# Both feed-forward products of a hybrid transformer layer, as seven half-size products each

## The chip, the cores and the metric

The kernel runs on one core of a Trainium2 chip, in one launch. Its metric is the device time in microseconds of that core; lower is better. Times of the kernel before: 2298.93 us in the median of three runs, from 2298.3 to 2300.44.

A core has a matrix engine (TensorE; PE in the profile, and PEld where it loads weights), three engines for elementwise work (VectorE or DVE, ScalarE or ACT, GpSimd or POOL), and SyncE (SP), which here only issues DMAs. Each works through its own queue in order and waits on semaphores. TensorE writes to PSUM, eight banks of 128 x 512 float32; everything else lies in SBUF or in DRAM.

## The reference

One layer on 1024 tokens of width 1024: a norm, three token mixers (a gated convolution, a stick-breaking attention, a cross-attention into 256 memory tokens) with sigmoid gates, an output projection, and the feed-forward block that this case is about. All in float32:

```python
merged = gates[:, :, 0] * y_conv + gates[:, :, 1] * y_sb + gates[:, :, 2] * y_x
x = x + merged @ w_out[l]

h2 = rms_norm(x, g_mlp[l])
x = x + jnp.square(jax.nn.relu(h2 @ w_up[l])) @ w_down[l]
```

`w_up` is 1024 x 4096 and `w_down` 4096 x 1024. The two products of the feed-forward block are 2 x 1024 x 1024 x 4096 multiply-adds.

## The kernel before

**Precision.** TensorE takes its operands in a rounded float32 type (`F32R`). To keep float32's accuracy every operand is split into a high part (a cast on ScalarE, lines 89 and 113) and a low part (the original less the high part, on VectorE, lines 90 and 114), and every product of tiles is three products: high x high, high x low, low x high (`mm3`, line 121, and `mm3_steps`, line 201, which does the same in steps between which other work is issued). A product is 128 x 128 by 128 x 512. I call the products that go into one PSUM bank one after the other a chain.

**Memory.** `pgp` holds 40 pages of 128 x 1024 float32 (`page`), `rawp` four raw weight tiles of that size (`load`, line 81, on the SP queue), `whlp` three pairs of split weights, `hpp` three half-width tiles. The PSUM banks are handed out as three `d`, two `z`, two `t` and one `o`.

**Order.** The program is written in one order, and a scheduler turns it into one queue per engine: it follows the written order where work is ready by its own estimate, and lets ready work pass work that waits. An instruction given to `keep_in_program_order` (line 93) stays behind those given to it earlier on its engine. Before, only the weight splits of the first stage were (`pin`).

**Stages.** Lines 316 to 723 make the projections, the attentions, the gates and the convolution. Lines 726 to 753 multiply the branches with the gates into `mT`. Lines 770 to 797 add `merged @ w_out` to `x`: `acc[t]`, eight tiles of 128 tokens, in two halves `ch` of the columns. In the second half every finished row block is normalized (`normed`, line 153: square and sum on ScalarE, a power on GpSimd, a scaling on VectorE), and the first four blocks are transposed on TensorE into `h2`, between the chains of the last three blocks (`norm_transpose`, line 172). `h2[k][th]` is block `k` of 128 model columns by half `th` of the tokens, high and low.

**Feed-forward, lines 800 to 835.** Eight chunks of 512 hidden columns. In a chunk, the up part makes four column blocks by two token halves, each a chain of 24 products (eight blocks `k`, three products), reads PSUM with a relu on ScalarE, squares and splits. The second half of the tokens is transposed between the products of the second chain of all. The down part runs over two halves of the output columns and eight token blocks, each a chain of 12 products, which VectorE adds to `acc[t]` (line 833); in the last chunk the sum goes out at once. Hidden values stay in SBUF.

Of the kernel before, what the change touches and what calls it, by code (L numbers as in the profile page):

```python
# [16 lines left out]
P = 128  # L17
# [5 lines left out]
NXH = 4  # L23
NM = M // P
FF = 4096
NCHUNK = FF // 512
EPS = 1e-6


# [7 lines left out]
def f32v(ap):  # L37

    return ap.bitcast(F32)
# [3 lines left out]
def block_kernel(ctx, tc, x, mem, small, w_in, w_v, w_kv, w_co, w_so, w_xo, w_out, w_up, w_dn, out):  # L43
# [19 lines left out]
    def page(dt=F32R, shape=(P, 1024)):  # L63
        return pgp.tile(list(shape), dt, tag="pg", name=nm("pg"))
# [41 lines left out]
    def unit(src, paged=False):  # L106

        return halves(load(src), paged)
# [63 lines left out]
    def norm_transpose(rows, dst, gcol):  # L172

        n = len(rows) * P
        for k in range(KT):
            tp = pt()
            for i, r in enumerate(rows):
                nc.tensor.transpose(tp[:, i * P : (i + 1) * P], r[:, k * P : (k + 1) * P], ident)
# [576 lines left out]

    acc = [None] * 8
    rows = []
    h2 = [None] * KT

    def h2_dst(th):  # L760
        def dst(k):
            if th == 0:
                h2[k] = {}
            t_ = page(F32R, (P, 2, 512))
            h2[k][th] = (t_[:, 0, :], t_[:, 1, :])
            return h2[k][th]

        return dst

    for ch in range(2):  # L770
        s = slice(ch * 512, ch * 512 + 512)
        while len(wo) < 4 * ch + 4:
            wo.append(unit(w_out[ch, len(wo) - 4 * ch], True))
        for t in range(8):
            th, i = t // 4, t % 4
            if ch == 0:
                acc[t] = page(F32)
                nc.sync.dma_start(out=acc[t], in_=x[t * P : (t + 1) * P, :])
            ps = pd()
            steps = mm3_steps(  # L780
                ps,
                [
                    (cut(mT[k, th], i * P, (i + 1) * P), cut(wo[4 * ch + k // 2], (k % 2) * 512, (k % 2) * 512 + 512))
                    for k in range(KT)
                ],
                4,
            )
            if ch == 1 and t == 5:
                more = norm_transpose(rows[0:4], h2_dst(0), C_GMLP)
            if ch == 1 and t >= 5:  # L790
                for _ in steps:
                    fill(more, 1)
            run(steps)
            nc.vector.tensor_tensor(out=acc[t][:, s], in0=ps, in1=acc[t][:, s], op=ALU.add)
            if ch == 1:
                rows.append(normed(acc[t]))
    run(more)


    for c in range(NCHUNK):  # L800
        f = {}
        for j2 in range(2):
            ws = [unit(w_up[4 * c + 2 * j2 + j]) for j in range(2)]
            for th, j in ((0, 0), (0, 1), (1, 0), (1, 1)):
                w = ws[j]
                ps = pd()
                steps = mm3_steps(ps, [(cut(w, k * P, (k + 1) * P), h2[k][th]) for k in range(KT)], KT)
                if (c, j2, th, j) == (0, 0, 0, 1):
                    weave(steps, norm_transpose(rows[4:8], h2_dst(1), C_GMLP))
                run(steps)  # L810
                r = hpp.tile([P, 512], F32, tag="hp", name=nm("r"))
                nc.scalar.activation(r, ps, AF.Relu)
                t_ = page(F32R, (P, 2, 512))
                f[2 * j2 + j, th] = (t_[:, 0, :], t_[:, 1, :])
                nc.scalar.activation(t_[:, 0, :], r, AF.Square)
                nc.vector.tensor_tensor(out=r, in0=r, in1=r, op=ALU.mult)
                nc.vector.tensor_tensor(out=t_[:, 1, :], in0=r, in1=f32v(t_[:, 0, :]), op=ALU.subtract)
        for ch in range(2):
            us = [unit(w_dn[c, ch, kp]) for kp in range(2)]
            s = slice(ch * 512, ch * 512 + 512)  # L820
            for t in range(8):
                ps = pd()
                mm3(
                    ps,
                    [
                        (
                            cut(f[j, t // 4], (t % 4) * P, (t % 4 + 1) * P),
                            cut(us[j // 2], (j % 2) * 512, (j % 2) * 512 + 512),
                        )
                        for j in range(4)  # L830
                    ],
                )
                nc.vector.tensor_tensor(out=acc[t][:, s], in0=ps, in1=acc[t][:, s], op=ALU.add)  # L833
                if c == NCHUNK - 1:
                    nc.sync.dma_start(out=out[t * P : (t + 1) * P, s], in_=acc[t][:, s])


def _layout(i):
# [10 lines left out]
    def per_part(v):  # L849
# [9 lines left out]
    w_dn = a["w_down"][0].reshape(NCHUNK, 2, 2, P, 2, 512).transpose(0, 4, 1, 3, 2, 5)  # L859
    return {  # L860
        "x": a["x"][0],
        "mem": a["mem"][0],
# [9 lines left out]
        "w_dn": w_dn.reshape(NCHUNK, 2, 2, P, 1024),  # L872
    }


# [17 lines left out]
```

## Time and profile before

| what | value |
|---|---|
| median of three runs | 2298.93 us |
| the profiled execution's time | 2298.66 us |
| its span, first to last instruction | 2297.0 us |
| TensorE busy | 2261.7 us (98%) |
| VectorE busy | 1127.5 us (49%) |
| ScalarE busy | 801.7 us (35%) |
| GpSimd busy | 298.2 us (13%) |
| granted TensorE clock, mean | 1.000 |
| DMA traffic | 174.79 MB, mean 76 GB/s |

The profile is one execution. A row of a group names the line, the engine, the operation, what it writes and reads, the shapes and the count; then the time that the engine was busy with it, the mean of one in ns, and the idle time ahead of it with what ended it. A row of the timeline gives start and duration in us, and in brackets the idle time ahead. TensorE's products overlap: the distance of two starts is what one costs, not its duration.

### The profile page before, as it was taken

What the parts mean: (1) busy time and instruction counts of PE and PEld (TensorE: products, weight loads), DVE (VectorE), ACT (ScalarE), POOL (GpSimd) and SP (SyncE); (2) the same over time, 40 slices, a digit from 0 to 9 for tenths busy, and PEclk for the clock granted to TensorE, in tenths of its full rate; (3) what the DMA queues carried; (4) which work ended last, traced back from release to release, by engine and by line L of the source; (5) the groups of instructions that cost most, each with busy time, mean ns of one, the idle gap of its engine ahead of it and who ended that gap; (6) DMA issues with size and microseconds to landing.
All of it is one profiled execution on the core that took longest, in us unless ns stands there. A gap on an engine that the chain in (4) does not pass through costs nothing.

```text
span 2297.0 us, 26957 instructions
## 1 busy us (share of the span) xinstructions
PE 2261.7 (98%) x10688; PEld 1882.5 (82%) x10688; DVE 1127.5 (49%) x1589; ACT 801.7 (35%) x1550; POOL 298.2 (13%) x422
## 2 busy tenths in 40 slices
PE   7999999999999999999999999999999999999999
PEld 7988888778788788888888888888888888888887
DVE  5533128787778778753333344434433333333333
ACT  6544226565555656532111121213221211221220
POOL 1021113333333333310000000000000000000000
PEclk9999999999999999999999999999999999999999
DMA  6311322222221222211112443250111111111111
GB/s 220 101 56 69 127 64 71 83 77 71 74 92 56 92 74 67 81 46 46 56 46 74 147 156 118 94 183 1 43 50 56 37 55 56 37 56 54 39 46 74
DMA packets 49455, 174.79 MB, mean 76 GB/s; under 512 B 6065, under 2 KB 6065, under 8 KB 49329
## 3 DMA queue, kind: packets, MB, share of 16 engines
q1 hardware_dynamic: 42160, 147.90, 20.5%
q0 software_dynamic: 7168, 25.17, 2.9%
q8 instruction: 84, 1.38, 0.2%
q14 instruction: 43, 0.34, 0.0%
HBM read 135.29 MB, written 29.36 MB: 72 GB/s over the span
## 4 chain that ended last, share of the span: by engine, by line
PE 85%; DVE 5%; issue 3%; ACT 3%; POOL 3%; DMA 1%; SPq 0%; POOLq 0%; ACTq 0%; DVEq 0%
PE d L207 17%; PE d L206 17%; PE d L205 17%; PE d L125 9%; PE d L126 9%; PE d L127 9%; POOL pg L558 2%; PE o L597 2%; DVE pg L114 1%; PE t L582 1%; DVE pg L572 1%; PE z L554 1%; PE z L553 1%; DVE whl L90 1%; ACT pg L555 1%
## 5 line engine op out<-in xcount | busy, mean ns | idle before, releaser
L205 PE MATMUL d<-pg,whl 128*128 128x512 f32 x1664 | 656.0, 394 | 0.0
L207 PE MATMUL d<-pg,whl 128*128 128x512 f32 x1664 | 649.1, 390 | 0.0
L206 PE MATMUL d<-pg,whl 128*128 128x512 f32 x1664 | 649.0, 390 | 0.0
L207 PEld LDWEIGHTS d<-pg,whl 128*128 128x128 f32 x1664 | 312.3, 188 | 66.5
L205 PEld LDWEIGHTS d<-pg,whl 128*128 128x128 f32 x1664 | 312.6, 188 | 60.6
L206 PEld LDWEIGHTS d<-pg,whl 128*128 128x128 f32 x1664 | 312.7, 188 | 60.4
L89 ACT CAST whl<-raw 128x1024 fp32r<-128x1024 f32 x160 | 168.6, 1054 | 518.4 <-PE d L127 306.6
L90 DVE TENSOR_TENSOR whl<-raw,whl 128x1024 fp32r<-128x1024 f32 x160 | 200.0, 1250 | 293.4 <-ACT whl L89 292.6
L558 POOL TENSOR_SCALAR_AFFINE_SELECT pg<-pg 128x128 f32<-128x128 f32 x256 | 167.9, 662 | 304.8 <-ACT pg L555 293.9
L568 DVE TENSOR_TENSOR_SCAN pg<-pg,zero 128x128 f32<-128x128 f32 (+7 forms) x128 | 177.4, 1386 | 57.4 <-POOL pg L558 54.7
L125 PE MATMUL d<-whl,pg 128*128 128x512 f32 x512 | 199.2, 389 | 0.0
L126 PE MATMUL d<-whl,pg 128*128 128x512 f32 x512 | 199.2, 389 | 0.0
L127 PE MATMUL d<-whl,pg 128*128 128x512 f32 x512 | 199.2, 389 | 0.0
L113 ACT CAST pg<-t 128x256 fp32r<-128x256 f32 (+2 forms) x336 | 115.2, 368 | 203.7 <-DVE pg L114 141.4
L833 DVE TENSOR_TENSOR pg<-d,pg 128x512 f32<-128x512 f32 x128 | 88.3, 690 | 188.7 <-PE d L127 188.5
L114 DVE TENSOR_TENSOR pg<-t,pg 128x256 fp32r<-128x256 f32 (+2 forms) x336 | 129.3, 404 | 65.5 <-ACT pg L113 62.0
L125 PE MATMUL d<-pg,whl 128*128 128x512 f32 x384 | 149.4, 389 | 0.0
L126 PE MATMUL d<-pg,whl 128*128 128x512 f32 x384 | 149.4, 389 | 0.0
L127 PE MATMUL d<-pg,whl 128*128 128x512 f32 x384 | 149.4, 389 | 0.0
L205 PE MATMUL d<-pg,pg 128*128 128x512 f32 (+1 forms) x384 | 138.5, 361 | 0.6 <-ACT pg L116 0.5
L206 PE MATMUL d<-pg,pg 128*128 128x512 f32 (+1 forms) x384 | 137.5, 359 | 0.5 <-DVE pg L90 0.5
L207 PE MATMUL d<-pg,pg 128*128 128x512 f32 (+1 forms) x384 | 137.5, 359 | 0.0
(114 smaller groups left out, 2755.4 us busy)
## 6 DMA issues: line engine op xcount, KB each, us to landing
raw<-in_w_in SPq DMA_DIRECT2D x72, 512.0 KB, 3.7
raw<-in_w_up SPq DMA_DIRECT2D x32, 512.0 KB, 3.6
raw<-in_w_dn SPq DMA_DIRECT2D x32, 512.0 KB, 4.1
gscr<-pg POOLq DMA_DIRECT2D x24, 512.0 KB, 3.0
raw<-gscr SPq DMA_DIRECT2D x24, 512.0 KB, 3.5
raw<-in_w_kv SPq DMA_DIRECT2D x16, 512.0 KB, 4.4
pg<-in_x SPq DMA_DIRECT2D x16, 512.0 KB, 8.7
pg<-pg SPq DMA_DIRECT2D x32, 256.0 KB, 4.0
```

The source lines that it names most:

```text
L89: a = nc.scalar.copy(hl[0], raw)
L90: b = nc.vector.tensor_tensor(out=hl[1], in0=raw, in1=f32v(hl[0]), op=ALU.subtract)
L113: nc.scalar.copy(hi, src)
L114: nc.vector.tensor_tensor(out=lo, in0=src, in1=f32v(hi), op=ALU.subtract)
L125: nc.tensor.matmul(ps, lhsT=ah, rhs=bh, start=i == 0, stop=False)
L126: nc.tensor.matmul(ps, lhsT=ah, rhs=bl, start=False, stop=False)
L127: nc.tensor.matmul(ps, lhsT=al, rhs=bh, start=False, stop=i == n - 1)
L205: nc.tensor.matmul(ps, lhsT=ah, rhs=bh, start=i == 0, stop=False)
L206: nc.tensor.matmul(ps, lhsT=ah, rhs=bl, start=False, stop=False)
L207: nc.tensor.matmul(ps, lhsT=al, rhs=bh, start=False, stop=i == n - 1)
L558: nc.gpsimd.affine_select(out=t_[:, W - P : W], in_=t_[:, W - P : W], pattern=[[-1, P]], compare_op=ALU.is_gt, fill=fill_, base=0, channel ...
L568: nc.vector.tensor_tensor_scan(out=rev, data0=rev, data1=zero.broadcast_to([P, W]), initial=1.0, op0=ALU.mult, op1=ALU.add)
```

## The change

Each of the two products is split into 2 x 2 blocks and made of seven block products in place of eight (Winograd's form of Strassen's scheme): operands are sums and differences of blocks, and results are sums of the seven products.

**Up** (`class Unit`). The weights are the first matrix: unit `u` pairs hidden column block `u` with `16 + u`, and each of the two with the lower and the upper half of the 1024 model columns (`a11`, `a12`, `a21`, `a22`). Of `h2` there are blocks 11, 21, 12, 22 (model half by token half) and four combinations `t1` to `t4`, made once: `h2_first` keeps the first token half raw and splits it, under the last `w_out` chains; `h2_second_a` makes `t1`, `t2`, and `h2_second_b` `t3`, `t4` and 22. A unit makes four weight combinations in `w2` and `w3` from raw weights, and splits them. Products `p1` to `p7` are chains of four blocks, 12 products each. Some chains go on in a bank whose state was copied out before: `p1`, `p6`, `p7`, `p4` share bank `a`, and `p5`, `p3` share `c`. Each of the four hidden results is relu'd and squared on ScalarE; `sums` makes the four combinations that the down product needs, and `put` stores all seven tiles unsplit to DRAM (`f_scr`) over the GpSimd queue. `acc` goes to DRAM too (`x_scr`), which frees its pages.

**Down.** 28 parts: four quarters `q` of the hidden blocks by seven products. Part `n` has four chains, one per block of 128 tokens, 12 products each; VectorE adds each chain to `acc`, and a bank goes on from one part to another of its set (`banks_a`, `banks_c`) as in the up half. `fetch(n + 2)` loads the stored hidden tiles and the blocks of `w_down` on the SP queue, `prep(n + 1, kp)` makes the combination of weight blocks and splits both operands while part `n` runs.

**Order.** Every elementwise instruction made by `vec` and `act`, and the first product of every chain, is given to `keep_in_program_order`. So the order on VectorE, on ScalarE and of the chains on TensorE is the written one. The diff, cut to its core:

```diff
-    for c in range(NCHUNK):
-        f = {}
...
+    def vec(out, a, op, b):
+        order(nc.vector.tensor_tensor(out=out, in0=a, in1=b, op=op))
+    def split_o(src, hi, lo):
+        act(hi, src)
+        vec(lo, src, ALU.subtract, f32v(hi))
+    def h2_second_a(rows, kk):
+        r0, r1, ta = h2_raw[kk], pair(), pair()
+        for j in range(2):
+            h2_tile(rows, kk + 4 * j, r1[:, j, :])
+        vec(ta[:, 0, :], r1[:, 0, :], ALU.subtract, r0[:, 0, :])
+        vec(ta[:, 1, :], r1[:, 1, :], ALU.subtract, ta[:, 0, :])
+        h2["t1"][kk], h2["t2"][kk] = split_pair(ta)
+        vec(r0[:, 0, :], r1[:, 1, :], ALU.subtract, r1[:, 0, :])
+        vec(r0[:, 1, :], r0[:, 1, :], ALU.subtract, ta[:, 1, :])
+        h2_new[kk] = r1
+    def h2_second_b(kk):
+        h2["t3"][kk], h2["t4"][kk] = split_pair(h2_raw[kk])
+        if kk % 2 == 0:
+            h2_22[:] = pair(F32R), pair(F32R)
+        j = kk % 2
+        h2["22"][kk] = tuple(t_[:, j, :] for t_ in h2_22)
+        split_o(h2_new[kk][:, 1, :], *h2["22"][kk])
...
             if ch == 1:
                 rows.append(normed(acc[t]))
+                nc.gpsimd.dma_start(out=x_scr[t], in_=acc[t])
...
+        def p2(self):
+            self.fa = pair()
+            c = pz()
+            chain_mm(c, col4(self.a12), h2["21"], first=True, last=True)
+            vec(self.fa[:, 0, :], c, ALU.add, self.x0)
+            self.relu2(self.fa[:, 0, :])
+        def p6(self):
+            chain_mm(self.a, col4(self.s2), h2["t2"])
+            self.xu = pair()
+            act(self.xu[:, 0, :], self.a)
...
+    U[0].load()
+    U[1].load()
+    U[0].w1()
+    U[1].w1()
+    for u in range(2):
+        h2_second_a(late, 2 * u)
+        U[u].p1(pd)
+        h2_second_a(late, 2 * u + 1)
+        U[u].p2()
+        U[u].w2()
+    for u in range(2):
+        h2_second_b(2 * u)
+        U[u].p6()
+        h2_second_b(2 * u + 1)
+        U[u].p5()
+    for u in range(NU):
+        un = U[u]
+        nx = U[u + 1] if u + 1 < NU else None
+        if u == 0:
+            un.w3()
+        if u < 2:
+            un.w4()
+        else:
+            un.p1(pd)
+            U[u - 1].sums()
+            un.w3()
+            un.p2()
+            un.w4()
+        if u + 2 < NU:
+            U[u + 2].load()
+        if u >= 2:
+            un.p6()
+            un.p5()
+        if u >= 1 and nx:
+            nx.w1()
+        un.p7()
+        if u == 0:
+            nx.w3()
+        elif nx:
+            nx.w2()
+        un.p3()
+        un.p4()
+        if u == 0:
+            un.sums()
+    U[NU - 1].sums()
...
+    fetch(0)
+    fetch(1)
+    prep(0, 0)
+    prep(0, 1)
+    for t in range(8):
+        acc[t] = page(F32)
+        nc.gpsimd.dma_start(out=acc[t], in_=x_scr[t])
+    for n in range(PARTS):
+        if n + 2 < PARTS:
+            fetch(n + 2)
...
+        for i in range(4):
+            chain_mm(
+                banks[i],
+                [cut(hl, i * P, i * P + P) for hl in fst[n]],
+                sec[n],
+                first=j in (0, 1, 5),
+                last=j in (3, 5, 6),
+            )
+            if n + 1 < PARTS and i % 2 == 0:
+                prep(n + 1, i // 2)
+            vec(acc[t0 + i][:, s], banks[i], ALU.add, acc[t0 + i][:, s])
```

The weights of the down product are laid out on the host as `(half of hidden, half of output, quarter, pair)` in place of `(chunk, half of output, pair)`.

More of the change, by code (lines that the diff above doesn't have):

```diff
@@ L25 @@
 FF = 4096
-NCHUNK = FF // 512
+NQ = 4
 EPS = 1e-6
@@ L757, in block_kernel @@
     rows = []
[L758 to L768, printed above, removed]
+    x_scr = [dram.tile([P, 1024], F32, name=f"xscr_{t}") for t in range(8)]
+    f_scr = {
+        (n, q): dram.tile([P, 4, 512], F32, name=f"fscr_{n}_{q}")
+        for n in ("11", "12", "22", "s1", "s2", "s3", "s4")
+        for q in range(NQ)
+    }
@@ new lines, in whl_pair, with chain_mm @@
+    def whl_pair(src):
+        w = whlp.tile([P, 2, 1024], F32R, tag="whl", name=nm("whl"))
+        split_o(src, w[:, 0, :], w[:, 1, :])
+        return [cut((w[:, 0, :], w[:, 1, :]), j * 512, j * 512 + 512) for j in range(2)]
+    def chain_mm(ps, a, b, first=False, last=False):
+        n = len(a)
+        for i, ((ah, al), (bh, bl)) in enumerate(zip(a, b)):
+            go = dict(skip_group_check=not first)
+            m_ = nc.tensor.matmul(ps, lhsT=ah, rhs=bh, start=first and i == 0, stop=False, **go)
+            if i == 0:
+                order(m_)
+            nc.tensor.matmul(ps, lhsT=ah, rhs=bl, start=False, stop=False, **go)
+            nc.tensor.matmul(ps, lhsT=al, rhs=bh, start=False, stop=i == n - 1, **go)
@@ new lines, in block_kernel, with h2_tile, h2_first @@
+    h2 = {n: [None] * 4 for n in ("11", "21", "22", "t1", "t2", "t3", "t4")}
+    h2_raw = [None] * 4
+    def h2_tile(rows, k, dst):
+        tp = pt()
+        for i, r in enumerate(rows):
+            nc.tensor.transpose(tp[:, i * P : (i + 1) * P], r[:, k * P : (k + 1) * P], ident)
+        nc.scalar.activation(dst, tp, AF.Copy, scale=sm[:, C_GMLP + k : C_GMLP + k + 1])
+    def h2_first(rows):
+        for kk in range(4):
+            h2_raw[kk] = pair()
+            for j in range(2):
+                h2_tile(rows, kk + 4 * j, h2_raw[kk][:, j, :])
+                yield
+            hi, lo = pair(F32R), pair(F32R)
+            split(flat(h2_raw[kk]), flat(hi), flat(lo))
+            h2["11"][kk], h2["21"][kk] = ((hi[:, j, :], lo[:, j, :]) for j in range(2))
@@ L788, in block_kernel @@
             if ch == 1 and t == 5:
-                more = norm_transpose(rows[0:4], h2_dst(0), C_GMLP)
+                more = h2_first(rows[0:4])
             if ch == 1 and t >= 5:
@@ L796, in block_kernel @@
                 rows.append(normed(acc[t]))
+                nc.gpsimd.dma_start(out=x_scr[t], in_=acc[t])
     run(more)
-    for c in range(NCHUNK):
-        f = {}
[L802 to L835, printed above, removed]
@@ new lines, in block_kernel @@
+    NU = 16
+    U = [Unit(u) for u in range(NU)]
+    late = rows[4:8]
+    U[0].load()
[42 more added lines that the diff above has]
+            un.sums()
```

138 lines of the change are left out of this document (136 added, 2 removed).

## The prediction, made before the changed kernel ran

> **What bounds the kernel now.** I read the page's engine line, then one window over the feed-forward stage, its groups, and rows of the timeline at its start and end.
>
> ```profile
> span 2297.0 us, 26957 instructions
> PE 2261.7 (98%) x10688; PEld 1882.5 (82%) x10688; DVE 1127.5 (49%) x1589; ACT 801.7 (35%) x1550; POOL 298.2 (13%) x422
> 1592.70:2292.82 700.12, 700.12 (x3105) 579.29 (x3103) 251.31 (x327) 142.33 (x199) 0.54 (x1) 1.00 0.16 49
> L205 PE MATMUL d<-pg,whl 128*128 128x512 f32 x512 | 199.9, 390 | 0.0
> L125 PE MATMUL d<-whl,pg 128*128 128x512 f32 x512 | 199.2, 389 | 0.0
> 1592.70 0.39 PE L205 MATMUL d<-pg,whl 128*128 128x512 f32 x1
> 1598.14 0.39 PE L205 MATMUL d<-pg,whl 128*128 128x512 f32 x1
> 2292.59 0.39 PE L127 MATMUL d<-whl,pg 128*128 128x512 f32 x1
> 2293.01 0.69 DVE L833 TENSOR_TENSOR pg<-d,pg 128x512 f32<-128x512 f32 x1 [2.03 <-PE d L127]
> ```
>
> In the window row PE, PEld, DVE, ACT and POOL follow the length of 700.12 us: PE has no gap, DVE works 251 us of it, ACT 142. Products overlap, so the mean of 389 ns is not their price: a chain of 24 starts at 1592.70, the next at 1598.14, and 5.44/24 = 0.2267 us. Six lines of 512 make 3072 products, 696.4 us; the other 3.7 us are 32 transposes. TensorE alone bounds this stage. I call 1592.70 the point zero, T.
>
> **What is removed.** Up: 16 units x 7 chains x 12 products = 1344 for 1536. Down: 28 parts x 4 chains x 12 = 1344 for 1536. 384 products x 0.2267 = **-87.0 us**, the most the change can give while pitch and cover hold. A chain now lasts 2.72 us, half of before.
>
> **What is added.** Each operation has a near row:
>
> ```profile
> L833 DVE TENSOR_TENSOR pg<-d,pg 128x512 f32<-128x512 f32 x128 | 88.3, 690 | 188.7 <-PE d L127 188.5
> L90 DVE TENSOR_TENSOR whl<-raw,whl 128x1024 fp32r<-128x1024 f32 x61 | 74.6, 1223 | 141.1 <-ACT whl L89 141.1
> L89 ACT CAST whl<-raw 128x1024 fp32r<-128x1024 f32 x61 | 63.9, 1047 | 286.4 <-PE d L127 286.4
> L816 DVE TENSOR_TENSOR r<-r 128x512 f32<-128x512 f32 x64 | 44.0, 688 | 112.8 <-ACT pg L815 112.8
> L815 ACT ACTIVATE pg<-r 128x512 fp32r<-128x512 f32 x64 | 40.3, 630 | 1.0
> L812 ACT ACTIVATE r<-d 128x512 f32<-128x512 f32 x64 | 38.3, 598 | 244.8 <-PE d L207 244.8
> 1613.02 0.60 ACT L812 ACTIVATE r<-d 128x512 f32<-128x512 f32 x1 [4.21 <-PE d L207]
> 1613.51 1.04 ACT L89 CAST whl<-raw 128x1024 fp32r<-128x1024 f32 x1
> 1614.58 1.23 DVE L90 TENSOR_TENSOR whl<-raw,whl 128x1024 fp32r<-128x1024 f32 x1 [4.19 <-ACT whl L89]
> ```
>
> Half-width VectorE step 0.69, full-width 1.23; ScalarE 0.60 out of PSUM, 0.63 in SBUF, 1.05 full-width. 1613.02 to 1613.51 shows that independent neighbours start 0.1 before the one ahead ends; the last two rows show a hand-over from ScalarE to VectorE of 0.03.
>
> *Up, per unit:* PE 84 x 0.2267 = 19.04 us. VectorE: three full splits, 12 half steps = 12.0. ScalarE: three full casts, 4 reads of PSUM, 8 half steps = 10.6. Neither is full, but their order is fixed, so look at the longest loop once it runs late: sum behind `p7`, two `w2` steps, cast, split, sum behind `p3`, relu, square, four `sums`, two `w3` steps, cast, split, sum behind `p2`, relu, square, `w4` cast, copy `xu0`, the 12 products of `p7` and 0.43 until their result can be read (2292.59 to 2293.01). That is 11 x 0.69 + 2 x 1.05 + 2 x 1.23 + 4 x 0.63 + 0.63 + 0.60 + 3.15 = 19.05, less some 0.7 for early starts: 18.4. It is under 19.04, by 3%: no stall in steady running, and lag is worked off slowly.
>
> *Down, per part:* PE 48 x 0.2267 = 10.88. VectorE: four additions 2.8, four splits 4.9, and in 16 of 28 parts two sums of weight blocks, after which it waits for a cast. Those parts take 2.6 + 2 x (1.23 + 1.05 + 1.23 + 1.2) = 12.0 in order, the others 7.4. Seven parts: 4 x 12.0 + 3 x 7.4 = 70.2 against 76.2. The first late part in a round may cost 0.5.
>
> *Stores and loads.* 112 quarter-megabyte stores and 16 transfers of `x_scr` go to the GpSimd queue, 56 reloads to SP beside the 64 weight loads that were there:
>
> ```profile
> L621 POOL DMA_DIRECT2D gscr<-pg x24: 548/571/582, 347.5 to 964.2; - x24
> oscr<-ox POOLq DMA_DIRECT2D x16, 256.0 KB, 2.3
> raw<-gscr SPq DMA_DIRECT2D x24, 512.0 KB, 3.5
> L83 SPq DMA_DIRECT2D raw<-gscr x24: 319/320/326, 1189.1 to 1481.5; - x24
> ```
>
> Issue is 7 x 0.57 = 4 us of a unit on a POOL that does 0.54 us in the stage, and 120 x 0.33 = 40 us of 640 on SP. Landing takes 2.3 to 3.5 us; a reload is issued two parts ahead, so some 10 us cover it. Priced at nothing; uncovered, a part would wait up to 3.5 us. The eight `x_scr` stores stand on POOL beside the power step of each row's norm; one ahead of the last row's would make it 0.57 later, but it is ready some 1.4 us sooner than that step. `acc` comes back during the last unit and the first 12 us of the down stage, before VectorE reaches the first addition; with that cover gone, 8 issues and a landing, about 8 us, would hold it. `h2_first` adds four casts and four splits (9.1 us) under the last `w_out` chains, where VectorE is free more than half of the time (without that cover, up to 9 us):
>
> ```profile
> 1550.00:1600.00 50.00, 50.00 (x240) 41.36 (x239) 18.81 (x33) 16.03 (x27) 4.39 (x8) 1.00 0.00 1
> ```
>
> **Where PE will stand: the first units.** Before, the late rows needed only a cast and a subtraction per tile. Now every `h2_second_a` is a chain through VectorE in fixed order.
>
> ```profile
> 1595.67 0.75 DVE L159 TENSOR_SCALAR pg<-pg,st 128x1024 f32<-128x1024 f32 x1 [0.66 <-POOL st L150]
> L116 ACT ACTIVATE pg<-t,sm 128x512 fp32r<-128x512 f32 x8 | 5.5, 687 | 2.8 <-PE t L178 2.8
> ```
>
> The last row block is scaled at 1596.42, T+3.7; transposes (0.6) and a copy (0.69) give the first tile at T+5.0. Then in VectorE's order: four `h2_second_a`, each 0.69 + 0.69 + 1.05 (waiting for the cast) + 1.23 + 2 x 0.69 = 5.05, 20.2; two `w2` at 3.7, 7.4; two sums, 1.4; four `h2_second_b` at 1.92, 7.7; `w3` of unit 0 until its cast, 2.4. While a split waits for its cast, the two subtractions behind it wait too, and behind those the sum of `p2`, the next `w2`, the next `h2_second_a`; for them wait `p6` and `p5`, which need the third operand of all four, and `p7`, which needs the last of `h2_second_b`. Sum: `p7` of unit 0 starts at T+44.1. PE has eight chains and the transposes until then, 21.8 + 3.7 = 25.5. Stall 18.6, plus 0.8 until the low half of `w3`. Bounds: 10, if casts overlap more than the order says, to 24, with 10% on every step. I take **+19.4**, which the rows give. Units 1 and 2 inherit the lag (`p4` waits behind the split for unit 2, `p7` behind a late `xu0`): **+1.7**, bounds 0 and 5.
>
> **Up to down.** `prep` of part 0 stands behind the last squares on ScalarE: 0.2 + 0.60 + 0.63, cast 1.05, then four splits of 1.23 less 0.3 of early starts: 7.1. The ninth product needs the last split and would start at 1.8: **+5.3**, bounds 3 and 8. **Down rounds: +0.5**, bounds 0 and 4.
>
> **The clock after a gap.** Rows of the kernel's own start:
>
> ```profile
> 7.81 0.69 PE L178 MATMUL t<-ident,pg 128*128 128x128 f32 x2 [7.81 <-DVE st L146]
> 10.90 0.42 PE L206 MATMUL d<-pg,pg 128*128 128x256 f32 x1
> 11.11 0.41 PE L205 MATMUL d<-pg,pg 128*128 128x256 f32 x1
> 18.43 0.28 PE L205 MATMUL d<-pg,pg 128*128 128x256 f32 x1
> 18.56 0.28 PE L206 MATMUL d<-pg,pg 128*128 128x256 f32 x1
> ```
>
> After 7.8 us of idling products of 256 columns start 0.21 apart, later 0.12: 1.75 times. Two gaps of 3 to 6 us lie on my path (ahead of `p7`, and at the down stage). If none cools the array it costs 0; if both do for two chains each, 2 x 2 x 2.72 x 0.75 = 8. I take **+2**, since the trace shows the slow pace only after a longer idle time. [...]
>
> **Sum.** -87.0 + 19.4 + 1.7 + 5.3 + 0.5 + 2 = -58.1. The profiled run took 2298.66 us (its span 2297.0 and 1.7 around it); 2298.66 - 58.1 = 2240.6. The median of 2298.93 is 0.3 above: I say **2241 us**.
>
> **Rivals.**
>
> *All hidden (5%).* If the scheduler moves work that is not pinned so that only half the first gap remains and the seam closes, -87.0 + 12: about 2224. Against: the steps in the chain are pinned.
>
> *The clock stays low (13%).* PE is sparse from T+15 to T+45 and may need long to recover: the 8 of above plus as much for units 1 and 2 give 2255.
>
> *The down stage is VectorE's (12%).* If a late part doesn't catch up because casts run only when VectorE asks, 16 x (12.0 - 10.9) = 18: 2258. Against: three parts in seven leave 3.5 us each.
>
> *Stores block VectorE (4%).* Rows beside POOL's work:
>
> ```profile
> 600.10 0.73 POOL L608 TENSOR_TENSOR pg<-tmp 64x256 f32<-64x256 f32 x1 [0.57 <-DVE tmp L607]
> 600.27 1.64 DVE L90 TENSOR_TENSOR whl<-raw,whl 128x1024 fp32r<-128x1024 f32 x1 [0.27 <-ACT whl L89]
> 598.98 0.55 POOL L621 DMA_DIRECT2D gscr<-pg  x1 [1.91 <-ACT pg L619]
> 598.51 0.82 DVE L572 TENSOR_TENSOR pg<-pg,pg 128x639 f32<-128x639 f32 x1
> 555.85 0.82 DVE L572 TENSOR_TENSOR pg<-pg,pg 128x639 f32<-128x639 f32 x1
> ```
>
> A GpSimd addition stretches a VectorE step from 1.23 to 1.64; a store's issue leaves one at 0.82, the same as without. If each of seven issues a unit held VectorE for its 0.57, the loop of 18.4 became 22.4: 14 x 3.4 = 47, 2288. [...]
>
> *Slower than before: the fixed order itself (6%).* If VectorE's and ScalarE's steps take 20% longer in their new forms (the row at 600.27 is 33% longer), the up loop is 22.1 (14 x 3.0 = 42), seven down parts take 84.2 against 76.2 (4 x 8 = 32), the start 9 more: 2241 + 83 = 2324. It decides from 3% in the up loop and 8% in the down rounds; slower than before from about 15%. Against: the nearest rows are the same operations on the same sizes.
>
> *It doesn't do what it says (2%)*: the products aren't fewer, or lost to waits one for one: about 2299.
>
> **How the numbers follow.** My forecast has 58%, with its own range of 2231 to 2252 from the bounds above. With the clock and the down stage, 83% lie between **2229 and 2266**. Under 0.2% (4.6 us) can't be told from no change here. Faster: all but the last two rivals, 0.92; same 0.02; slower 0.06.
>
> **What would show it.** 2688 products of 512 columns still 0.227 apart; PE idle about 19 us in the first 55 of the stage, released by VectorE splits; some 5 us ahead of the first down part, released by the casts and splits of `prep`; no idle time in units 4 to 14 nor for long in the down parts; VectorE near 63% in the up stage. I am wrong if PE waits in every unit or part, if VectorE's full-width steps exceed 1.3, or if PE waits for a DMA.

## The result, and the profile after

The changed kernel takes 2242.27 us in the median of four runs (2241.97 to 2243.7), against 2299.64 (2298.3 to 2300.44) for the kernel before beside it: a ratio of 0.9752, 95% interval 0.9735 to 0.9769. Five more runs of it, on another occasion, gave 2242.45 against 2298.33: 0.9756 (0.9743 to 0.9769). The forecast was 2241, inside 2229 to 2266.

The page of the changed kernel, its span and its engine line:

```profile
span 2242.0 us, 27020 instructions
PE 2187.6 (98%) x10304; PEld 1817.1 (81%) x10304; DVE 1310.4 (58%) x1781; ACT 948.3 (42%) x1726; POOL 367.4 (16%) x550
```

Its windows over the whole feed-forward stage and over 100 us in the steady part of the up half (columns: window, length, busy time and instructions of PE, PEld, DVE, ACT and POOL, then granted clock, DMA share, GB/s), and from the groups of the down half, ahead of the | shapes and count, behind it busy us and mean ns, the commonest new step:

```profile
1593.74:2237.46 643.72, 624.77 (x2721) 512.75 (x2719) 438.84 (x526) 288.17 (x374) 65.60 (x122) 0.98 0.46 154
1700.00:1800.00 100.00, 100.00 (x443) 82.81 (x442) 59.93 (x82) 53.11 (x78) 21.47 (x40) 1.00 0.46 156
```

```profile
L774 DVE TENSOR_TENSOR pg<-pg,pg 128x1024 fp32r<-128x1024 f32 x52 | 63.5, 1221 | 34.3 <-ACT pg L777 34.3
```

The 384 products are gone (10304 for 10688) and 192 VectorE instructions are new. In the steady part TensorE has no gap, with VectorE at 60% of the time. VectorE's work in the stage has gone from 251 to 439 us, and a full-width step still takes 1.22. Over the whole stage TensorE now lacks 19 us in idle time, and the mean clock is 0.98. What the change costs stands at the start of the stage and at the passage from up to down. TensorE's timeline there, in order of time; the brackets give the idle time ahead:

```profile
1593.51 0.39 PE L207 MATMUL d<-pg,pg 128*128 128x512 f32 x1
1593.74 0.82 PE L819 MATMUL t<-ident,pg 128*128 128x128 f32 x6
...
1598.54 0.69 PE L819 MATMUL t<-ident,pg 128*128 128x128 f32 x2 [3.99 <-DVE pg L159]
...
1622.64 0.79 PE L806 MATMUL d<-pg,whl 128*128 128x512 f32 x1 [2.96 <-ACT pg L777]
...
1639.08 0.80 PE L806 MATMUL d<-pg,whl 128*128 128x512 f32 x1 [4.42 <-ACT whl L777]
...
1644.72 0.39 PE L806 MATMUL z<-pg,whl 128*128 128x512 f32 x1
...
1656.28 0.47 PE L806 MATMUL d<-pg,pg 128*128 128x512 f32 x1 [0.49 <-DVE pg L774]
...
1670.94 0.50 PE L806 MATMUL d<-pg,whl 128*128 128x512 f32 x1 [0.80 <-ACT pg L777]
...
1926.54 0.39 PE L810 MATMUL d<-pg,pg 128*128 128x512 f32 x1
...
1930.16 0.50 PE L806 MATMUL d<-pg,whl 128*128 128x512 f32 x1 [3.24 <-ACT whl L777]
...
1931.61 0.79 PE L810 MATMUL d<-pg,whl 128*128 128x512 f32 x1 [0.64 <-DVE whl L774]
...
2237.23 0.39 PE L810 MATMUL o<-pg,pg 128*128 128x512 f32 x1
```

The out-projection's last product starts at 1593.51, so the stage begins at 1593.74; `p7` of unit 0 starts at 1639.08, 45.3 us behind that, and the chain takes 5.64 us (to 1644.72) where twelve products at 0.227 take 2.72. From the stage's begin to its last product are 643.5 us; before, they were 2292.59 - 1592.70 = 699.9. The stage is 56.4 shorter. In the profiled execution it also began 1.0 later, in a part of the program that the change doesn't touch; the profiled runs of this study have that point between 1591.3 and 1594.3, and no cause was sought.

### The profile page after: what moved, and what is told of

Its sections match the earlier page's. It is cut to its first block, busy times and chain, and to the rows that moved or that the text cites. A ratio compares the mean times of both kernels' runs of the same rounds, so it can differ in the third digit from the quotient of the medians.

```text
span 2242.0 us, 27020 instructions
## 1 busy us (share of the span) xinstructions
PE 2187.6 (98%) x10304; PEld 1817.1 (81%) x10304; DVE 1310.4 (58%) x1781; ACT 948.3 (42%) x1726; POOL 367.4 (16%) x550
## 4 chain that ended last, share of the span: by engine, by line
PE 80%; DVE 7%; ACT 4%; issue 4%; POOL 3%; DMA 0%; POOLq 0%; DVEq 0%; ACTq 0%; SPq 0%
PE d L205 12%; PE d L207 12%; PE d L206 12%; PE d L810 4%; PE d L806 4%; PE d L125 4%; PE d L127 4%; PE d L809 4%; PE d L126 4%; PE z L806 3%; PE z L809 3%; PE z L810 3%; POOL pg L558 2%; PE o L597 2%; DVE pg L114 1%
## 5 line engine op out<-in xcount | busy, mean ns | idle before, releaser
L205 PE MATMUL d<-pg,whl 128*128 128x512 f32 x1152 | 456.4, 396 | 0.0
L207 PE MATMUL d<-pg,whl 128*128 128x512 f32 x1152 | 449.9, 390 | 0.0
L206 PE MATMUL d<-pg,whl 128*128 128x512 f32 x1152 | 449.7, 390 | 0.0
L777 ACT ACTIVATE pg<-pg 128x512 f32<-128x512 f32 (+2 forms) x180 | 140.2, 782 | 295.9 <-DVE pg L774 293.9
L207 PEld LDWEIGHTS d<-pg,whl 128*128 128x128 f32 x1152 | 216.2, 188 | 47.0
L205 PEld LDWEIGHTS d<-pg,whl 128*128 128x128 f32 x1152 | 216.5, 188 | 40.9
L206 PEld LDWEIGHTS d<-pg,whl 128*128 128x128 f32 x1152 | 216.6, 188 | 40.5
L90 DVE TENSOR_TENSOR whl<-raw,whl 128x1024 fp32r<-128x1024 f32 x96 | 121.7, 1268 | 152.4 <-ACT whl L89 151.6
L89 ACT CAST whl<-raw 128x1024 fp32r<-128x1024 f32 x96 | 101.5, 1058 | 228.4 <-PE d L207 82.6
L774 DVE TENSOR_TENSOR pg<-pg,pg 128x1024 fp32r<-128x1024 f32 (+3 forms) x144 | 149.6, 1043 | 64.4 <-ACT pg L777 63.1
L125 PE MATMUL d<-pg,whl 128*128 128x512 f32 x384 | 149.4, 389 | 0.0
L126 PE MATMUL d<-pg,whl 128*128 128x512 f32 x384 | 149.4, 389 | 0.0
L127 PE MATMUL d<-pg,whl 128*128 128x512 f32 x384 | 149.4, 389 | 0.0
L806 PE MATMUL d<-pg,whl 128*128 128x512 f32 x288 | 115.3, 401 | 11.8 <-ACT whl L777 7.7
L809 PE MATMUL d<-pg,whl 128*128 128x512 f32 x288 | 114.8, 398 | 1.2 <-DVE pg L774 1.2
```

What stands on the lines that cost most here:

```text
L125: nc.tensor.matmul(ps, lhsT=ah, rhs=bh, start=i == 0, stop=False)
L126: nc.tensor.matmul(ps, lhsT=ah, rhs=bl, start=False, stop=False)
L127: nc.tensor.matmul(ps, lhsT=al, rhs=bh, start=False, stop=i == n - 1)
L205: nc.tensor.matmul(ps, lhsT=ah, rhs=bh, start=i == 0, stop=False)
L206: nc.tensor.matmul(ps, lhsT=ah, rhs=bl, start=False, stop=False)
L207: nc.tensor.matmul(ps, lhsT=al, rhs=bh, start=False, stop=i == n - 1)
```

## The experiments

| run | what it is | us, median | range | ratio to the kernel before, 95% |
|---|---|---|---|---|
| after | the changed kernel | 2242.27 | 2241.97 to 2243.7 | 0.9735 to 0.9769 |
| e1 | first down part made in the last units | 2251.8 | 2250.51 to 2251.85 | 0.9782 to 0.9812 |
| e2 | two subtractions between cast and split | 2238.67 | 2236.19 to 2239.86 | 0.9725 to 0.9754 |
| e3 | stores on the SP queue | 2249.78 | 2249.5 to 2251.88 | 0.9773 to 0.9806 |
| e4 | order left to the scheduler | 2240.96 | 2239.91 to 2242.09 | 0.9737 to 0.9766 |
| e5 | three more VectorE steps per unit | 2270.57 | one run | |
| e6 | the two long waits filled with products | 2239.58 | 2239.01 to 2241.03 | 0.973 to 0.9761 |
| e8 | e1, and acc back earlier | 2241.46 | 2240.96 to 2243.8 | 0.974 to 0.9771 |
| e9 | e8, its parts earlier still, and e2 | 2238.96 | 2235.84 to 2240.29 | 0.9727 to 0.9762 |
| e10 | start and seam in a new order | 2226.83 | 2222.03 to 2227.96 | 0.9668 to 0.97 |
| e11 | e10, one step moved | 2224.63 | 2221.29 to 2226.01 | 0.9664 to 0.969 |
| e12 | waits of graded length | 2269.03 | one run | |

### The start: is it VectorE's order?

The prediction's theory of the 45.3 us is a written order in which each split waits for its own cast and all that stands behind it waits too. e2 exchanges neighbours in that order, in `h2_second_a`, and nothing else:

```diff
-        h2["t1"][kk], h2["t2"][kk] = split_pair(ta)
+        hi, lo = pair(F32R), pair(F32R)
+        act(flat(hi), flat(ta))
         vec(r0[:, 0, :], r1[:, 1, :], ALU.subtract, r1[:, 0, :])
         vec(r0[:, 1, :], r0[:, 1, :], ALU.subtract, ta[:, 1, :])
+        vec(flat(lo), flat(ta), ALU.subtract, f32v(flat(hi)))
...
```

> Edit: in each of the four steps h2_second_a the two later subtractions are written between the cast and the subtraction that waits for it. Same work, other order. Theory (the start is bound by VectorE's order, with 1.1 us of idle time per step for the cast): 4 x 1.1 = 4.5 us less, about 2238; p7 of unit 0 starts 4 to 5 us sooner. Rival (the start is bound by VectorE's amount of work, or by ScalarE): no change, 2242.

TensorE's timeline of e2, the out-projection's last product and `p7` of unit 0:

```profile
1592.51 0.39 PE L207 MATMUL d<-pg,pg 128*128 128x512 f32 x1
...
1634.29 0.50 PE L806 MATMUL d<-pg,whl 128*128 128x512 f32 x1 [3.07 <-ACT whl L777]
```

`p7` comes 41.6 us behind the stage's begin (1592.74), 3.7 sooner than 45.3: some 0.9 for each of the four casts. The median is 3.6 under that of the changed kernel. The same number of steps, the same work, another order.

e4 takes the order away: `order` returns its instruction as it is, and the scheduler places all of it.

```diff
-    order = tc.keep_in_program_order
+    def order(i):
+        return i
```

> Edit: no instruction of the feed-forward block is held to the written order; the scheduler places all of them by its own estimates. Theory (the written order leaves no stall in units 4 to 15 and in the down parts, and costs some 20 us at the start): the start may gain up to 10 us, since splits may move up into idle time, and the steady halves can only lose; between 2232 and 2262. Rival (the fixed order itself costs time in steady running): faster than 2230.

It took 2240.96, which its interval does not tell from the changed kernel. The scheduler's start is the better one (TensorE's waits there come to 8.3 us in place of 13.8) and its passage to the down stage the worse one (11.3 in place of 3.9); that passage is told of below.

### How much room the written order has in a steady unit

e5 repeats the last subtraction of `sums` three times more in every unit (`for _ in range(4)` ahead of it).

> The last subtraction of the four sums of a unit (the operand s4) is done four times over, into the same tile: three half-width VectorE steps of 0.60 to 0.69 us more in every unit, nothing else. Theory (the prediction's longest loop through one unit, 18.4 us in program order against 19.04 us of products): three steps make the loop 20.2 to 20.5, so each of 14 steady units gets 1.2 to 1.5 us longer: +15 to +22 us, some 2260, and TensorE shows an idle time in every unit, released by VectorE. Rival (only the busy share counts; VectorE is busy 60% of a unit and the steps lift it to 70%): the time of the changed kernel, 2242, and no idle time in units 3 to 14.

Its VectorE timeline shows the four steps in one unit, TensorE's the waits in two units that follow each other, and the view of waits those of the window 1680 to 1948 (us in total, times, the longest):

```profile
1808.77 2.87 DVE L774 TENSOR_TENSOR xh<-pg,pg 128x512 f32<-128x512 f32 x4
```

```profile
1672.92 0.50 PE L806 MATMUL d<-pg,whl 128*128 128x512 f32 x1 [1.42 <-ACT pg L777]
...
1693.67 0.50 PE L806 MATMUL d<-pg,whl 128*128 128x512 f32 x1 [1.39 <-ACT pg L777]
```

```profile
PE d L806 <- ACT pg L777: 18.1, 13, 1.4
```

Thirteen waits of 1.39 us, one a unit, where the changed kernel has none: the loop in the written order is the bound, and VectorE's share (60% before, 65% with the steps) is not. The 2260 expected was too low, mainly because a step that writes the tile of the step before it does not start early: four take 2.87, so each repeat costs (2.87 - 0.69)/3 = 0.73 and not the 0.60 at which independent neighbours start (1808.17 and 1808.77 in the same timeline). Three cost 2.18. The unit has become 1693.67 - 1672.92 = 20.75 us, so the loop without the repeats is 18.6: against 19.04 of products that is a margin of 0.4 to 0.5 us, 2%, where the prediction had 18.4 and 3%. One more half-width step a unit, 0.60 to 0.73, about uses it up.

### The stores and the queue

e3 issues the 112 stores on SP, where the loads stand, in place of GpSimd:

```diff
-            nc.gpsimd.dma_start(out=f_scr[n, self.u // 4][:, self.u % 4, :], in_=t_)
+            nc.sync.dma_start(out=f_scr[n, self.u // 4][:, self.u % 4, :], in_=t_)
```

> Edit: the 112 stores of hidden tiles are issued on the SP queue in place of the GpSimd queue. Theory (stores cost VectorE nothing, and the loads on SP have slack): within 2 us of 2242, VectorE's steps unchanged. Rival A (store issue on GpSimd holds VectorE back): faster, up to 0.57 us x 7 x 16 = 60 us if each issue stopped it, and shorter VectorE steps in the up half. Rival B (loads on SP get stuck behind stores that wait for a sum): slower by several us per unit.

7.3 to 7.5 us slower, and not spread over the units: those run as before. SP's timeline at the passage, and then ScalarE's and TensorE's:

```profile
1923.95 0.37 SPq L1050 DMA_DIRECT2D pg<-in_w_dn  x1
1926.92 1.65 SPq L987 DMA_DIRECT2D fscr_s<-pg  x3
1928.66 0.45 SPq L987 DMA_DIRECT2D fscr<-pg  x1
1929.21 0.54 SPq L987 DMA_DIRECT2D fscr_s<-xh  x1
1929.84 3.21 SPq L1050 DMA_DIRECT2D pg<-in_w_dn  x3
```

```profile
1931.99 1.06 ACT L777 ACTIVATE pg<-pg 128x1024 fp32r<-128x1024 f32 x1 [3.86 <-DMA pg<-in_w_dn]
```

```profile
1934.05 0.79 PE L806 MATMUL d<-pg,whl 128*128 128x512 f32 x1 [7.21 <-ACT whl L777]
```

Three loads of weight blocks stand on SP behind stores that wait for the last unit's results; the cast of the first part waits for a load, and TensorE's wait is 7.21 us where it was 3.24. On GpSimd's queue the stores have nothing behind them that is needed soon in this kernel; the return of `acc`, which does stand there, is told of below. Of the fourth rival, stores that hold VectorE, nothing is seen: the half-width steps into `xh` in the changed kernel, eleven of them beside 76 issues of GpSimd in 200 us, are alike to 2 ns at 681 to 683, and the half-width steps of the kernel before (line 816), with one instruction of GpSimd in the whole stage, take 688 in the mean. The row of that tile in the changed kernel gives count, then duration in ns, least, median and most:

```profile
L774 DVE TENSOR_TENSOR xh<-pg,pg x11: 681/683/683, 1701.3 to 1891.7; 128x512 f32<-128x512 f32 x11
```

### The clock behind a wait

The chain of `p7` took 5.64 us. e6 puts 16 products that nobody reads into the wait ahead of it and 12 into the wait at the passage, in a spare bank (`warm(16)` ahead of the unit loop, `warm(12)` behind it).

> In the two long waits of the changed kernel (ahead of the third product of unit 0's second half, p7, and ahead of the first down part) TensorE gets products that nobody reads: 16 and 12 products of 512 columns into a spare bank. The added products change no result. Theory (the slow pitch of 0.427 us behind the waits of 4.4 and 3.2 us comes from the wait itself): with the wait filled, p7 of unit 0 and the first down part run at 0.227 from their first product: the 24 or so slow products gain 0.2 each, 2.8 + 1.4 less 0 to 1 for the fill ending late: 2238 to 2239. Rival (the pitch is slow because operands come late, not because of the clock): the pitch stays 0.427 behind the fill and the time is 2242 or, with the fill in the way, up to 2245.

The changed kernel's window over the chain of `p7`, and behind it the same window of e6:

```profile
1630.00:1645.00 15.00, 10.55 (x35) 7.73 (x34) 9.59 (x13) 7.45 (x12) 0.00 (x0) 0.77 0.22 70
```

```profile
1630.00:1645.00 15.00, 14.48 (x63) 11.40 (x62) 10.43 (x14) 8.32 (x13) 0.54 (x1) 1.00 0.27 74
```

The granted clock is 1.00 in place of 0.77, `p7` starts at the same 45.3 behind the begin, and its chain ends 2.0 us sooner. 2.7 to 2.9 us less in the median: the slow pitch is the clock's, not the operands'. At the full clock the chain still takes 3.63 us for 2.72, since its third product waits for the low half of `w3`, as e6's timeline of TensorE shows:

```profile
1638.88 0.50 PE L810 MATMUL d<-pg,whl 128*128 128x512 f32 x1 [0.52 <-DVE whl L774]
```

e12 asks how long the wait must be. It repeats the same subtraction as e5 in every other unit only, 3, 4, 5, 6, 7 and 8 times more.

> Waits of graded length in the steady up stage, to see after how short a wait TensorE's products come at the slow pitch of 0.427: the last subtraction of the four sums is done 3, 4, 5, 6, 7 and 8 times more in units 3, 5, 7, 9, 11 and 13 (0.60 us each), with an ordinary unit after each to recover. In the runs so far waits of 0.4 to 1.7 us kept the pitch at 0.227, waits of 1.9 us and more did not, each followed by some 3 us of products at 0.427. Theory A (a wait of about 2 us is enough): waits of some 1.0, 1.6, 2.2, 2.8, 3.4 and 4.0 us; behind those above 2 us a slow stretch of 3 to 5 us, 1.5 to 2.5 us each, none behind the shorter ones: 2242 + 15 + 4 x 2 = 2265. [...]

TensorE's timeline, the first product behind each of the six waits, and the windows that begin at the third and the fourth (the clock is the third number from the end):

```profile
1708.74 0.50 PE L806 MATMUL d<-pg,whl 128*128 128x512 f32 x1 [1.40 <-ACT pg L777]
...
1749.23 0.50 PE L806 MATMUL d<-pg,whl 128*128 128x512 f32 x1 [2.13 <-ACT pg L777]
...
1790.47 0.50 PE L806 MATMUL d<-pg,whl 128*128 128x512 f32 x1 [2.85 <-ACT pg L777]
...
1832.43 0.50 PE L806 MATMUL d<-pg,whl 128*128 128x512 f32 x1 [3.58 <-ACT pg L777]
...
1876.76 0.79 PE L806 MATMUL d<-pg,whl 128*128 128x512 f32 x1 [4.30 <-ACT pg L777]
...
1922.41 0.74 PE L806 MATMUL d<-pg,whl 128*128 128x512 f32 x1 [5.02 <-ACT pg L777]
```

```profile
1790.47:1795.00 4.53, 4.53 (x20) 3.75 (x21) 2.85 (x5) 2.09 (x4) 0.00 (x0) 1.00 0.60 174
1832.43:1838.00 5.57, 5.57 (x17) 4.42 (x18) 2.52 (x4) 1.77 (x3) 0.00 (x0) 0.69 0.37 141
```

In this run theory A does not fit: waits of 2.13 and 2.85 us between busy stretches leave the clock at 1.00, and one of 3.58 does not (0.69 in its window). All six waits were longer than expected, since a repeat costs 0.73 us and not 0.60, and the last three were followed by slow products: 20.2 us lost at the waits and some 6 by slow products make 2242.4 + 26 = 2268 of the 2269.0 measured.

But this is one execution, and other traces of this study show the slow pace behind shorter waits. In e5 a wait of 2.65 us, behind 10.5 us without a gap, was followed by slow products (clock 0.58). The row of the first of them, and e5's window from there:

```profile
1656.09 0.76 PE L806 MATMUL d<-pg,pg 128*128 128x512 f32 x1 [2.65 <-DVE pg L774]
```

```profile
1656.05:1660.00 3.95, 3.91 (x11) 3.13 (x12) 2.79 (x4) 2.25 (x3) 0.54 (x1) 0.58 0.55 220
```

Two short waits close together were enough in e10 and in e11 (the order changed once more, below). Behind these two, in e11's timeline, products came 0.43 apart until 1620.77:

```profile
1616.09 0.49 PE L806 MATMUL d<-pg,whl 128*128 128x512 f32 x1 [1.17 <-ACT pg L777]
1617.35 0.64 PE L809 MATMUL d<-pg,whl 128*128 128x512 f32 x1 [0.77 <-DVE pg L774]
```

In the feed-forward stages of all the traces every wait of 3.07 us or more was followed by slow products, no wait of up to 1.73 us that stood alone was, and between these lengths there are both cases (slow behind 1.89 us in e10 and 2.65 in e5, not behind 2.13 and 2.85 in e12). It also differs from execution to execution: of the four of e10, and of the four of e11, the fastest (2222.03 and 2221.29) had a mean granted clock of 1.000 and the others of 0.997 or 0.998. So theory A does not hold as a rule, the expectation's reading that waits of up to 1.7 us keep the pitch holds for lone ones only, and what decides between the two lengths no run settles.

The first two waits and their lengths also give the loop once more: each further repeat makes the wait 0.73 longer, and three, 2.18 us, make 1.56 of lost time (1.40 and 0.16 behind it), so the margin is 0.6 there, in a unit that runs without lag.

### The passage from up to down: three bounds in a row

e1 makes the first down part's operands earlier: `fetch(0)` and `fetch(1)` where the last two units load no weights, `prep(0, 0)` behind `p7` and `prep(0, 1)` behind `p3` of the last unit.

```diff
+        else:
+            fetch(u + 2 - NU)
...
+        if not nx:
+            prep(0, 0)
         un.p3()
+        if not nx:
+            prep(0, 1)
         un.p4()
...
-    fetch(0)
-    fetch(1)
-    prep(0, 0)
-    prep(0, 1)
```

> Edit: the loads and the two operand steps of down part 0 are written into the last two up units, ahead of the last two chains, in place of behind them. Theory (PE stands at the seam because part 0's casts and splits are queued behind the last squares): the gap of 3.4 us, the 1.2 us of waits inside the first chain and the slow pace behind it (some 1.4 us) go; 6 us less, about 2236. Rival (the seam waits for the return of acc or for loads, which crowd together there at 340 GB/s): the gap stays, 2241 to 2243.

It was 9.5 us slower than the changed kernel. TensorE's wait ahead of the first part is 2.51, but there is a new one of 7.80 in front of the second; VectorE's timeline of e1 names its cause:

```profile
1940.44 0.69 DVE L774 TENSOR_TENSOR pg<-d,pg 128x512 f32<-128x512 f32 x1 [2.53 <-DMA pg<-xscr]
1947.07 0.69 DVE L774 TENSOR_TENSOR pg<-d,pg 128x512 f32<-128x512 f32 x1 [5.94 <-DMA pg<-xscr]
```

```profile
1929.37 0.51 PE L806 MATMUL d<-pg,pg 128*128 128x512 f32 x1 [2.51 <-ACT pg L777]
...
1950.98 0.80 PE L806 MATMUL z<-pg,pg 128*128 128x512 f32 x1 [7.80 <-ACT pg L777]
```

VectorE's first additions wait 2.5 and 5.9 us for `acc` to come back from `x_scr`, and the sum of weight blocks for the next part stands behind them. The eight reloads were issued from 1931.3 to 1944.2, in place of 1930.2 to 1935.9. GpSimd's timeline puts the waits between them down to stores and reloads still under way and, once, to a product that reads its operands, so to pages not yet free; that the operands made earlier are what keeps the pages is argued from this, and e8 tests it. e4 shows the same bound from the other side, VectorE there being early; its VectorE timeline:

```profile
1929.32 0.69 DVE L775 TENSOR_TENSOR pg<-d,pg 128x512 f32<-128x512 f32 x1 [7.53 <-DMA pg<-xscr]
```

The prediction put the return of `acc` at nothing, as hidden, and at about 8 us without its cover: the cover is VectorE's own lateness, and without it VectorE waits 7.5. What was off is the landing: these eight take 12.4 us from issue to landing in the median of the changed kernel, where the prediction took 3.5 at most. e8 is e1 with the reloads ahead of the last unit's stores, behind its `p5`, where the pages of four used operands come free:

```diff
             un.p6()
             un.p5()
+        if not nx:
+            for t in range(8):
+                acc[t] = page(F32)
+                nc.gpsimd.dma_start(out=acc[t], in_=x_scr[t])
```

> As the run that moved the first down part's loads and splits into the last up units (2251.8, with a wait of 7.8 us ahead of the second part's products), and beside that the eight reloads of acc from x_scr are issued on the GpSimd queue behind p5 of the last unit, ahead of that unit's stores, instead of behind them. Theory (in that run VectorE's first addition waited 2.5 and 5.9 us for acc, and the splits of the next part stood behind it): acc lands some 10 us earlier, the 7.8 us go and with them some slow products, 2240 to 2243; with the 2.5 us wait of the first part left. Rival (the queue is full there: 13 MB in 40 us, 320 to 420 GB/s in most slices): the wait only moves to the loads of the first parts, and the time stays at 2249 to 2252.

GpSimd's timeline of e8 shows seven reloads issued at once, 13 us earlier than in e1; TensorE's shows what is left:

```profile
1917.83 3.69 POOL L1077 DMA_DIRECT2D pg<-xscr  x7
```

```profile
1928.33 0.51 PE L806 MATMUL d<-pg,pg 128*128 128x512 f32 x1 [2.52 <-ACT pg L777]
...
1942.75 0.50 PE L810 MATMUL z<-pg,pg 128*128 128x512 f32 x1 [0.63 <-DVE pg L774]
```

10.3 us less than e1; the wait for `acc` is gone. But it is not told apart from the changed kernel, since the first part still waits 2.52. In e9 that part's casts and splits stand one place earlier still, and e2's edit is in it.

> The edit before this one with the first down part's casts and splits one step earlier still (ahead of p7 and p3 of the last unit, where the operands of a next unit would be made), and with the two subtractions of the first unit's r0 put between a cast and its split, as in the run that gave 2238.7. Theory (the seam is a matter of what VectorE and ScalarE have in hand when the last up product ends, and of acc): no wait over 1 us at the seam, 5.9 us less there and 3.6 less at the start: 2232 to 2235. Rival (loads bound the seam): 2240 to 2248, with waits released by transfers.

The first part waits for nothing. The second does now, 2.48 us, in e9's TensorE timeline:

```profile
1935.39 0.53 PE L806 MATMUL z<-pg,pg 128*128 128x512 f32 x1 [2.48 <-ACT pg L777]
```

On VectorE `prep` of the second part stands behind the four sums of the last unit, and in it each split behind its own cast (two waits of 1.1). 2238.96 is a miss against the 2232 to 2235 expected, and within its spread what e2 alone gave; neither theory as it was put holds, since the wait was again the order and not a transfer.

### All of it in a new order

e10 keeps the work and changes where it stands. At the start: `w1` of units 0 and 1 and `w2` of unit 0 under the last `w_out` chains; `p1` of unit 0 ahead of the late transposes and three more chains between them; three subtractions between each cast and its split; first what `p6` and `p5` need, then `t3`, `t4`, 22. At the passage: e9, all four casts of a down part ahead of its splits, and the last unit's sums inside the first part. Its core:

```diff
+    A.p1(pd)
+    A.x0copy()
+    late_tiles(late, 0)
+    A.p2()
+    late_ta(0)
+    late_r(0)
+    late_tiles(late, 1)
+    B.p1(pd)
+    late_lo(0)
+    late_ta(1)
...
+                if i == 0:
+                    ready = [prep(n + 1, 0), prep(n + 1, 1)]
+                if i in (1, 2):
+                    ready[i - 1]()
+                if n == 0 and i == 2:
+                    U[NU - 1].sums()
```

> Everything that the runs so far say of the two waits, put together. Start: a cast and the split that needs it no longer stand side by side in the order of any engine; the three subtractions after a cast, or the next row tile's, stand between them; w2 of unit 0 is made during the last w_out chains; the first product p1 of unit 0 and then p2 and p1 of unit 1 go between the late transposes; the operands t3, t4 and 22 come after the ones that p6 and p5 need. Seam: as the run before (first part's operands and acc early), the casts of a down part all ahead of its splits, and the four sums of the last unit inside the first down part. Theory (both waits are VectorE's program order and the waits for casts in it, not its work): VectorE has some 28 us of steps for p7 of unit 0 and starts them 5 us after the out-projection's last product, so p7 starts at about 32 to 34 us behind it instead of 45.3; no wait over 1 us at the seam. 2242 - 12 - 5.9 - 1.4 to 2.8 for the slow products = 2221 to 2225. Rival (the work itself, or the pages that it needs, sets the start): p7 at 40 or later and 2232 to 2239, as the run before.

2226.83: 15.4 us under the changed kernel, and 3.2% under the kernel before. `p7` of unit 0 stands 37.3 behind the begin, between the two theories; what held it was a sum behind `p2` of unit 1, too late among VectorE's steps, which empties the bank that `p5` of unit 1 needs. e11 moves that one step to stand behind the sum for unit 0.

> One step of the run before (2226.8) moved: the sum behind p2 of unit 1 stands right behind that of unit 0, not behind seven later VectorE steps. In that run p5 of unit 1 waited 1.89 us for its PSUM bank, which this sum empties, and the products behind it ran 0.43 apart for 3 us. Theory (the wait and the slow pitch behind it are both that step's place): p7 of unit 0 at 33 to 34 us behind the out-projection instead of 37.3, 3 to 3.7 us less in all: 2223 to 2224. Rival (VectorE only gets to its next step later, and another product waits as long): within 1 of 2227.

TensorE's timeline of e11, the out-projection's last product and `p7`, and its window over the passage:

```profile
1594.07 0.39 PE L207 MATMUL d<-pg,pg 128*128 128x512 f32 x1
...
1627.68 0.39 PE L806 MATMUL d<-pg,whl 128*128 128x512 f32 x1
```

```profile
1905.00:1955.00 50.00, 50.00 (x222) 41.42 (x221) 41.03 (x46) 26.10 (x32) 8.05 (x15) 1.00 0.79 286
```

`p7` starts 33.4 us behind the begin, without a wait, as the first theory had it, and the passage has no gap at all. The median is 2224.63, a ratio of 0.9677 (0.9664 to 0.969). The 2.2 us between e10 and e11 are less than the 5 us over which the runs of each spread, so the times alone don't tell the two apart; the 3.9 us that `p7` comes earlier do.

Beside e11 the changed kernel ran again:

> The changed kernel itself, beside the run above, on the same chip: 2242 by its four runs so far; some 2 us of its profiled run lie ahead of the feed-forward stage, where nothing was changed, and need not come again: 2240 to 2243.

2242.45 (2241.71 to 2242.79): e11 is 17.8 us faster, and no run of the one reaches into those of the other.

## Why the prediction was right

By its own terms, in us; what was measured is read from the rows above.

| term | predicted | measured |
|---|---|---|
| 384 products | -87.0 | -87.0, pitch still 0.227 |
| ahead of `p7` of unit 0, and until the low half of `w3` | +19.4 | +20.7 |
| lag in units 1 and 2 | +1.7 | +1.6 |
| up to down | +5.3 | +4.3 |
| down rounds | +0.5 | 0 |
| clock behind a gap | +2 | +3.5 |
| sum | -58.1 | -56.9 |

The stage by itself became 56.4 shorter, so 0.5 is not accounted for. The terms are each right to within 1.5 us, but +1.3 and +1.5 stand against -1.0, -0.5 and -0.1; that the whole came within 1.3 us of the median is in part luck.

*The start.* 45.3 less the 25.5 of chains and transposes that TensorE does in that time is 19.8; with the 0.9 that e6 shows for the low half of `w3` it is 20.7, where the prediction had 18.6 and 0.8. Not all of the 19.8 is idle time: the trace shows 13.8 of waits, and the rest is mostly products that ran slow behind the first of them; these cost nothing by themselves, since `p7` waits for VectorE. The prediction had `p7` at 44.1. The 1.2 between them lies ahead of the first subtraction, which started at 1600.67, 6.9 behind the begin in place of 5.0; the steps after it took 0.7 less than priced. Of the 1.9, some 0.9 are the `w1` splits of two units, which had been placed between the last row's scaling and that subtraction. The other 1.0 is the `x_scr` store, which stood on GpSimd right ahead of the last row's power. The prediction said that this store would be ready some 1.4 us sooner than that power; GpSimd's timeline shows otherwise:

```profile
1596.53 0.58 POOL L885 DMA_DIRECT2D xscr<-pg  x1 [5.53 <-DVE st L146]
1597.13 0.57 POOL L150 TENSOR_TENSOR st<-st,mhalf 128x1 f32<-128x1 f32 x1
```

By the profile the very step that the power waits for released the store, and the store went first, so that claim of the prediction failed. The power starts 1.09 behind the end of the step that it waits for, in place of 0.08 before. That the mechanism is the order, e2, e10 and e11 show: 45.3, 41.6, 37.3 and 33.4 with the same steps, some of which e10 and e11 place ahead of the stage's begin.

*Units 1 and 2.* The lost time ahead of the rows at 1656.28 and 1670.94 is 0.65 and 0.95, 1.6 together, with the releasers that the prediction named.

*Up to down.* 3.39 and 0.88 were lost there, 4.3, plus the slow products that stand under the clock. The prediction's chain (last squares, cast, four splits) is what the waits show; its 5.3 was too long by 1.0, and it did not see what e1 and e4 brought to light, that `acc`'s return stood just behind it.

*The clock* is the term that was most mis-sized. The prediction took 2 of a possible 8, "since the trace shows the slow pace only after a longer idle time". The chain of `p7` lost 2.9 (5.64 for 2.72), of which 0.9 is the low half of `w3` and 2.0 the clock, and the first down part lost 1.5 (seven products from 1931.61 on, some 0.2 longer each). Together they make 3.5, between the 2 taken and the 8 possible. The runs bear that reason out in part: every wait of 3.07 us or more was followed by the slow pace, but some shorter ones were too (1.89 us in e10, 2.65 in e5).

*The steady units and the down parts.* No wait of TensorE from unit 3 on; the 3% of margin is 2 to 3% by e5 and e12. The down rounds needed nothing: VectorE is busy for 76 to 78 of 100 us there and TensorE doesn't wait.

*The rivals.* "All hidden" is what e10 and e11 come near to, by another written order; the scheduler alone, in e4, shortened the waits at the start and lengthened those at the passage. The clock did not stay low: every slow stretch ends within 7 us of the last wait ahead of it (2.3 in e9 to 6.9 in the changed kernel's second trace). Stores blocking VectorE, and steps that get longer in the new forms, are excluded by the 0.68 to 0.69 and 1.22 us of the new steps. The down stage was not VectorE's.

## What to carry to other kernels

In an order fixed by hand, price the loop through all engines, waits for casts included, and not the shares; and put independent steps between a cast and the step that needs it, since there alone 3.7 us lay in two exchanged lines. Where a term is put at nothing because it is hidden, write down what hides it: two repairs of the visible wait at the passage gained nothing until the reload behind it, and then the next part's operands, were moved as well. A queue that waits in order should hold nothing behind a store that someone needs soon: in e3 that made a wait of 3.24 us one of 7.21.

## What the runs showed of the hardware that was not expected

- TensorE's pace is about halved (0.427 for 0.227 us) for some 2 to 7 us behind a wait, and no single length decides: every wait of 3.07 us or more did it, of lone ones between products 2.65 us did it (e5) and 2.13 and 2.85 did not (e12), and two of 1.17 and 0.77 close together were enough. The same kernel can show more of it in one execution than in the next (e10 and e11: a mean clock of 1.000 in one of four, of 0.997 or 0.998 in the others). Products that nobody reads kept the clock up (e6: 1.00 in place of 0.77 from 1630 to 1645).
- A half-width VectorE step that writes the same tile as the one before it cost 0.73 us in a row (e5, e12), against 0.60 for independent neighbours (e5).
- On GpSimd's queue and on SP's a DMA that waited for its data held what stood behind it: TensorE's wait at the passage grew from 3.24 to 7.21 us in e3, and one power of a norm came 1.0 us later in the changed kernel.
